# A hybrid decoder block on one core: split weights kept in DRAM for later blocks, LRU gates by heads of 64 rows, mixed input units, gelu in one operation

## The chip, the core and the metric

One NeuronCore of a Trainium2 chip runs the whole kernel. Its engines work side by side and wait for each other by semaphores: TensorE (PE, matrix products; its weight loads are listed as PEld), VectorE (DVE, elementwise), ScalarE (ACT, copies and functions), GpSimd (POOL, little used here) and SyncE (SP), whose queue issues every DMA in order. Tiles live in SBUF (128 partitions); matmuls accumulate in PSUM. The metric is the device time of one execution in microseconds; lower is better.

## The reference

The input is 2048 tokens of width 1024 in float32, one layer:

```
h = rmsnorm(x, norm_mix_g)
gate_b, gate_c, v, x_r, g = split(h @ w_in, [512, 1024, 1536, 2560])
y_conv = gate_b * causal_dwconv(gate_c * v, conv_w)
xr = causal_dwconv(x_r, rnn_conv_w) + rnn_conv_b
y_rnn = rg_lru(xr, w_a, b_a, w_x, b_x, lru_lambda) * gelu(g)
x = x + concat([rmsnorm(y_conv), rmsnorm(y_rnn)]) @ w_out
z = square(relu(rmsnorm(x) @ w_mlp_in))
out = rmsnorm(x + z @ w_mlp_out)
```

rg_lru computes two sigmoid gates, r and i, from xr with block-diagonal weights: 16 heads, each a 64 x 64 matrix for w_a and one for w_x. From r and lru_lambda it makes a decay a and a factor sqrt(1 - a*a), and scans h[t] = a*h[t-1] + factor*i*xr over the sequence.

## The kernel before

**Precision.** Each float32 operand of a product is split into a high part (a cast to fp32r, `w_hi`, `h_hi`, ..., on ACT) and the rest (a subtraction on DVE, `w_lo`, `h_lo`, ...): `split_into`, L152 to L154. A product is three matmuls, hi x hi, hi x lo and lo x hi (`passes`, L186).

**Blocks.** The sequence is cut into four blocks of 512 tokens, in two pairs. For each block `mixers` (L966) computes the two mixers and `w_out_rows` and `w_out_conv` (L992, L1014) the product with w_out; after both blocks of a pair the MLP runs on the pair with a seven-product Strassen scheme (`Up` and `Down`, L708 to L905).

**Units.** w_in and w_out are taken in units of 256 columns or rows, 1 MB each, 20 per block: x0 g0 x1 g1 x2 g2 x3 g3, then c, v, b for two column pairs, then oB0 to oB3 and oA0, oA1 of w_out. Each unit is 48 matmuls of 512 columns. `take` (L174) hands out a unit, issues the loads of the ones after it (`load_unit`, raw tiles of 512 KB from DRAM) and the splits of the next two (`split_unit`). Raw and split tiles share a pool of 15 slots of 4 KB per partition (`wp`), so a load waits until an older unit's slots are free. In every block the same 20 units are loaded raw and split anew.

**A mixer pair.** For each of four pairs `pr` of 128-channel groups, `lru_conv` (L550) copies the x unit's result out of PSUM, convolves it on DVE and splits it into xr_hi and xr_lo; `lru_gelu` (L584) makes the polynomial of the tanh gelu from the g unit's result; `lru_scan` (L598) does the gate products. `load_gates` (L272) builds two 128 x 1024 tiles, one for w_a and one for w_x, with two heads on the diagonal of each 128 x 128 square and zeros beside them; per 128 channels six matmuls (L610, accumulator `psri`) use all 128 rows. Then come sigmoids, tanh, exp and sqrt on ACT and the scan on DVE. In block 0 the results are scaled by `row` on DVE.

**Norms.** `next_part` (L929) prepares the next block's norm in steps; its step 8 spreads four scales over the partitions with a matmul (L380) into a PSUM tile `bc` of its own, and ACT copies that to `bcs`. `stats` (L532) sums squares over channels with four matmuls (L536) into a tile `sps`.

**What sets the order.** Outside of parts that are written out by hand, a scheduler orders each engine's instructions by estimated times; the program order sets what exists. Within an engine, instructions start in order, and a wait holds back all that is behind it. All tiles come from rings of slots: PSUM has four accumulators of two banks (`psp`).

**Start of the MLP.** `seq` (L1118) runs products 1 and 2 of three column slices first. Meanwhile `rest` (L1102) turns the last tiles of the second block and makes H6 and H5, and H7, H3 and H4 are split at steps 2, 3 and 4. `Up.drain` adds and squares the results (L789, L797, L801, square at L780) and stores them (`d_z`); `Down.fetch` loads them back, `Down.prepare` splits them.

Of the kernel before, what the change touches and what calls it, by code (L numbers as in the profile page):

```python
# [50 lines left out]
def block_kernel(  # L51
# [75 lines left out]
    units = []  # L127
    for b in range(NB):
        for pr in range(4):
            units.append(("x%d" % pr, src_col(w_in, COL_X + 256 * pr)))  # L130
            units.append(("g%d" % pr, src_col(w_in, COL_G + 256 * pr)))
        for pr in range(2):
            for nm, col in (("c", COL_C), ("v", COL_V), ("b", COL_B)):
                units.append((nm + str(pr), src_col(w_in, col + 256 * pr)))
# [17 lines left out]
    def split_into(hi, lo, src, lo_engine=None):  # L152
        nc.scalar.copy(hi, src)  # L153
        (lo_engine or V).tensor_tensor(lo, src, hi.bitcast(F32), SUB)  # L154
# [111 lines left out]
    def gate_tiles():  # L266
        raw = [temp("gate_raw", (P, NLRU, P)) for _ in range(2)]
        for r in raw:
            nc.gpsimd.memset(r, 0.0)
        return raw  # L270

    def load_gates(raw):  # L272
        res = []
        for src, r in zip((w_a, w_x), raw):
            sv = src[0].rearrange("(c e) i j -> e i c j", e=2)
            for e in range(2):
                nc.sync.dma_start(
                    r[64 * e : 64 * e + 64, :, 64 * e : 64 * e + 64], sv[e]
                )
            hi = temp("gate_hi", (P, NLRU, P), F32R)  # L280
            lo = temp("gate_lo", (P, NLRU, P), F32R)
            split_into(hi, lo, r)
            res.append((hi, lo))
        return res
# [34 lines left out]
    for nm, n in ROWS:  # L319
        nc.sync.dma_start(prow[o : o + n, :], srcs[nm])  # L320
# [161 lines left out]
    l_neg = cp.tile(L8, F32, name="l_neg")  # L482
    l_abs = cp.tile(L8, F32, name="l_abs")
    l_u = cp.tile(L8, F32, name="l_u")
    l_d = cp.tile(L8, F32, name="l_d")
    l_w = cp.tile(L8, F32, name="l_w")
    l_w2 = cp.tile(L8, F32, name="l_w2")
    l_s = cp.tile(L8, F32, name="l_s")
# [2 lines left out]
    V.tensor_scalar(l_neg, lam, -1.0, 0.0, MUL, MAX)
    V.scalar_tensor_tensor(l_abs, l_neg, 2.0, lam, MUL, ADD)
    nc.scalar.activation(l_u, l_abs, AF.Exp, scale=-1.0)
    V.tensor_scalar(l_d, l_u, 2.0, None, ADD)
    V.reciprocal(l_d, l_d)
    V.tensor_mul(l_w, l_u, l_d)
    V.tensor_mul(l_w2, l_w, l_w)
    V.tensor_scalar(l_s, l_w2, 2.0 / 15, 2.0 / 13, MUL, ADD)
    for n in (11, 9, 7, 5, 3, 1):
        V.tensor_mul(l_s, l_s, l_w2)  # L500
        V.tensor_scalar(l_s, l_s, 2.0 / n, None, ADD)
    V.tensor_mul(l_s, l_s, l_w)
    V.tensor_add(l_s, l_s, l_neg)
# [750 lines left out]
```

## Time and profile before

| | |
|---|---|
| median of three runs | 2193.27 us (2191.85 to 2193.27) |
| profiled execution | 2192.01 us |
| its span, first to last instruction | 2190.2 us |
| granted TensorE clock, mean | 0.997 |
| bytes moved by DMA | 334.10 MB, 153 GB/s in the mean |
| matmuls | 9634 |

The page gives for each engine the time in which it was busy, the groups of instructions by line and tile, and the chain of work that ended last. A group's row holds line, engine, operation, tiles written and read, shape and count, then total busy time and the mean of one in ns, then the idle time before them and what ended it. Matmuls overlap: one lasts longer than the distance to the next, so their pace is read from starts, as in the chain's pieces. The slices of the page show the clock in tenths, and 9 or more in all of them.

### The profile page before, as it was taken

The page shows a single profiled execution, that of the slowest core. Times are in us where ns is not written, and L with a number is a line of the kernel's source. Part 1 is how long each engine was busy: PE and PEld are TensorE (multiplying, and loading weights), DVE is VectorE, ACT ScalarE, POOL GpSimd, SP SyncE. Part 2 cuts the span into 40 slices and gives each one's busy share as a digit, 9 for nine tenths or more (in the row PEclk, how much of TensorE's full clock was granted, in tenths as well). Part 3 has the DMA queues.
Part 4 walks back from the last instruction along what each step waited for, and adds up shares of the span by engine and source line. Part 5 has one row for each costly group of instructions (what it writes and reads, how often), then busy time and mean ns, then how long its engine had stood idle before and what let it go on. Part 6 is the DMA issues. An engine that isn't in the chain of part 4 may idle for free.

```text
span 2190.2 us, 25124 instructions
## 1 busy us (share of the span) xinstructions
PE 2168.8 (99%) x9634; PEld 1793.4 (82%) x9634; DVE 1671.5 (76%) x1951; ACT 1033.0 (47%) x1341; POOL 52.0 (2%) x54
## 2 busy tenths in 40 slices
PE   9999999999999999999999999999999999999997
PEld 7888888887888888888888888888888888788886
DVE  7898678769757678778888876876886665887866
ACT  6764486534333333334478535774443333333343
POOL 0110001000000000000000000000000000000000
PEclk9999999999999999999999999999999999999999
DMA  7334533443453577444263424233335355854432
GB/s 250 105 117 154 183 106 125 146 133 108 148 177 116 203 270 257 154 154 145 89 210 93 158 97 163 87 127 142 106 118 200 116 186 198 304 195 154 132 100 77
DMA packets 179752, 334.10 MB, mean 153 GB/s; under 512 B 14672, under 2 KB 104880, under 8 KB 179632
## 3 DMA queue, kind: packets, MB, share of 16 engines
q1 hardware_dynamic: 179632, 332.49, 44.2%
q8 instruction: 76, 1.25, 0.2%
q14 instruction: 44, 0.36, 0.0%
HBM read 252.76 MB, written 79.69 MB: 152 GB/s over the span
## 4 chain that ended last, share of the span: by engine, by line
PE 88%; DVE 7%; DMA 2%; issue 1%; SPq 1%; ACT 0%; POOL 0%; DVEq 0%; ACTq 0%; POOLq 0%
PE dn L878 27%; PE up L764 23%; PE po L217 11%; PE ps_g L193 7%; PE ps_x L193 7%; PE ps_b L193 4%; PE ps_c L193 3%; PE ps_v L193 3%; PE psri L610 2%; DVE w_lo L154 1%; DVE H L154 1%; DMA x<-in_x_dram 1%; DVE x L922 0%; PE tps L1010 0%; DVE snap L789 0%
## 5 line engine op out<-in xcount | busy, mean ns | idle before, releaser
L764 PE MATMUL up<-H,w_hi 128*128 128x512 f32 x1792 | 552.4, 389 | 1.3 <-DVE snap L789 1.3
L764 PEld LDWEIGHTS up<-H,w_hi 128*128 128x128 f32 x1792 | 335.8, 188 | 72.0 <-issue 2.5
L878 PE MATMUL dn<-w_lo,z_hi 128*128 128x512 f32 x896 | 349.4, 390 | 1.9 <-DVE w_lo L154 1.9
L878 PE MATMUL dn<-w_hi,z_hi 128*128 128x512 f32 x896 | 349.3, 390 | 0.0
L878 PE MATMUL dn<-w_hi,z_lo 128*128 128x512 f32 x896 | 349.2, 390 | 0.0
L764 PE MATMUL up<-H,w_lo 128*128 128x512 f32 x896 | 348.7, 389 | 0.3 <-DVE w_lo L154 0.3
L153 ACT CAST w_hi<-w 128x1024 fp32r<-128x1024 f32 x156 | 164.2, 1052 | 339.2 <-PE up L764 159.4
L154 DVE TENSOR_TENSOR w_lo<-w,w_hi 128x1024 fp32r<-128x1024 f32 x156 | 190.5, 1222 | 111.6 <-ACT w_hi L153 39.3
L154 DVE TENSOR_TENSOR w_lo<-raw,w_hi 128x1024 fp32r<-128x1024 f32 x158 | 192.3, 1221 | 89.3 <-ACT w_hi L153 39.1
L153 ACT CAST z_hi<-z 128x1024 fp32r<-128x1024 f32 x112 | 117.8, 1051 | 200.1 <-PE dn L878 158.2
L153 ACT CAST w_hi<-raw 128x1024 fp32r<-128x1024 f32 x158 | 163.6, 1046 | 102.9 <-PE po L217 64.5
L878 PEld LDWEIGHTS dn<-w_lo,z_hi 128*128 128x128 f32 x896 | 168.6, 188 | 38.0 <-DVE w_lo L154 2.8
L764 PEld LDWEIGHTS up<-H,w_lo 128*128 128x128 f32 x896 | 168.2, 188 | 35.6 <-DVE w_lo L154 0.8
L878 PEld LDWEIGHTS dn<-w_hi,z_lo 128*128 128x128 f32 x896 | 168.6, 188 | 35.0
L878 PEld LDWEIGHTS dn<-w_hi,z_hi 128*128 128x128 f32 x896 | 168.5, 188 | 35.0
L154 DVE TENSOR_TENSOR z_lo<-z,z_hi 128x1024 fp32r<-128x1024 f32 x112 | 136.7, 1221 | 58.7 <-issue 26.1
L890 DVE TENSOR_TENSOR x<-dn,x 128x1024 f32<-128x1024 f32 x112 | 136.5, 1221 | 20.8 <-PE dn L878 20.6
L217 PE MATMUL po<-w_hi,y_hi 128*128 128x512 f32 x384 | 119.4, 392 | 0.0
L217 PE MATMUL po<-w_lo,y_hi 128*128 128x512 f32 x384 | 118.3, 389 | 0.0
L217 PE MATMUL po<-w_hi,y_lo 128*128 128x512 f32 x384 | 118.3, 389 | 0.0
L193 PE MATMUL ps_x<-h_hi,w_hi 128*128 128x512 f32 x240 | 93.5, 390 | 0.0
L193 PE MATMUL ps_g<-h_hi,w_hi 128*128 128x512 f32 x240 | 93.5, 390 | 0.0
(235 smaller groups left out, 3562.8 us busy)
## 6 DMA issues: line engine op xcount, KB each, us to landing
raw<-in_w_in_dram SPq DMA_DIRECT2D x112, 512.0 KB, 3.7
z<-d_z SPq DMA_DIRECT2D x112, 512.0 KB, 4.4
w<-in_w_mlp_in_dram SPq DMA_DIRECT2D x64, 512.0 KB, 6.7
d_z<-snap SPq DMA_DIRECT2D x64, 512.0 KB, 3.6
raw<-in_w_out_dram SPq DMA_DIRECT2D x48, 512.0 KB, 3.5
d_z<-z SPq DMA_DIRECT2D x48, 512.0 KB, 4.8
w<-in_w_mlp_out_dram SPq DMA_DIRECT2D x48, 512.0 KB, 3.6
x<-in_x_dram SPq DMA_DIRECT2D x20, 512.0 KB, 8.0
```

The source lines that it names most:

```text
L153: nc.scalar.copy(hi, src)
L154: (lo_engine or V).tensor_tensor(lo, src, hi.bitcast(F32), SUB)
L193: nc.tensor.matmul(ps[:, j, lo:hi], ws[k // 4][:, k % 4, j * P : (j + 1) * P], hs[:, k, lo:hi], start=k == 0 and i == 0, stop=k == KD - 1 ...
L217: nc.tensor.matmul(ps[:, half, :], ys[:, j, t * P : (t + 1) * P], ws[j][:, 0, half * 512 : (half + 1) * 512], start=first and i == 0, stop ...
L610: nc.tensor.matmul(pr_[:, half, :], ws[:, c, :], xsrc[:, j, :], start=i == 0, stop=i == len(pl) - 1,)
L764: nc.tensor.matmul(ps[:, j, :], ws[:, k, j * P : (j + 1) * P], hs(k), start=i in (1, 2, 5) and k == 0 and n == 0, stop=k == 3 and n == len ...
L878: nc.tensor.matmul(ps[t // 2][:, t % 2, :], zs[:, p, t * P : (t + 1) * P], ws[:, p, :], start=i in (1, 2, 5) and a == 0 and p == 0 and n == 0,
L890: V.tensor_add(xt[b, th, dh], ps[th], xt[b, th, dh])
```

## The change

It makes six edits.

1. **Kept splits.** When a unit is taken for the first time (units 3 to 22: the rest of block 0, and the first three of block 1), its four split tiles are stored to DRAM (`put_by`). A later block loads these four tiles straight into split slots, 2 MB per unit, with no cast and no subtraction, and looks two units ahead instead of three.
2. **Gates by heads.** One raw tile holds both weights: on rows 0 to 63 the even heads' w_a and w_x side by side, on rows 64 to 127 the odd heads' w_x and w_a. A matmul uses one half of the rows (64 of contraction, 128 results: 64 channels of r and 64 of i); the two halves alternate and have one PSUM bank each. The sigmoids work on 64 partitions, and b_x is needed with its halves swapped.
3. **Order of units.** x0 g0 x1 c0 g1 x2 v0 g2 x3 b0 g3 c1 v1 b1. The gate products follow the next pair's x unit; scan and convolution stand apart.
4. **gelu** in one ACT operation (`Gelu_apprx_tanh`) instead of square, tanh and three DVE operations.
5. **w_out.** The norm's spread and the sums of squares move from the mixers into the start of `w_out_rows`, where they use the fourth accumulator `po[3]` ahead of its own products; the splits of y are made one unit ahead.
6. **Start of the MLP.** For three of the eight slices relu and square run on ACT (two operations) instead of DVE (one). Two transposed tiles instead of one are left for the first MLP steps, H7, H3 and H4 are split at steps 4, 5 and 6, and the first Down operands are fetched a step earlier. In block 0 the split of the gates and the softplus of lru_lambda stand behind the first xr_lo.

```diff
+def KEEP(u, n):
+    return 3 <= u < n + 3
+    UNITS = ("x0", "g0", "x1", "c0", "g1", "x2", "v0", "g2", "x3", "b0", "g3", "c1", "v1", "b1")
+    def put_by(u, tiles):
+        cache[u % NU] = []
+        for part in tiles:
+            row = []
+            for t in part:
+                d = dp.tile(list(t.shape), F32, name="d_w")
+                nc.sync.dma_start(d, t.bitcast(F32))
+                row.append(d)
+            cache[u % NU].append(row)
     def load_unit(u):
...
+        his, los = [], []
+        for hi_d, lo_d in zip(*cache[u % NU]):
+            for to, d, nm in ((his, hi_d, "w_hi"), (los, lo_d, "w_lo")):
+                t = wtile(nm, shape, F32R)
+                nc.sync.dma_start(t.bitcast(F32), d)
+                to.append(t)
+        splits[u] = (his, los)
     def take(nm, ahead=AHEAD, lo_engine=None):
...
-        if ahead:
+        if ahead and not (u + ahead + 1 < len(units) and is_kept(u + ahead + 1)):
             load_unit(u + ahead + 1)
...
+        if KEEP(u, NU):
+            put_by(u, splits[u])
+    def load_gates():
+        r = temp("gate_raw", (P, NLRU, P))
+        for e in range(2):
+            for g, src in enumerate((w_a, w_x)):
+                col = 64 * ((g + e) % 2)
+                sv = src[0].rearrange("(c e) i j -> e i c j", e=2)
+                nc.sync.dma_start(r[64 * e : 64 * e + 64, :, col : col + 64], sv[e])
+        return r
     def lru_gelu(pr, h, row=None):
-            nc.scalar.copy(g, psg)
-            nc.scalar.activation(s, psg, AF.Square)
+            nc.scalar.activation(s, psg, AF.Gelu_apprx_tanh)
...
-        V.tensor_scalar(s, s, 0.044715, 1.0, MUL, ADD)
-        V.tensor_mul(s, s, g)
+    def lru_gates(pr, xr, xr_hl, gs):
-            for half, wg in enumerate(gates):
-                pl = passes(wg, xr_hl)
-                for i, (ws, xsrc) in enumerate(pl):
+            heads = (slice(0, 64), slice(64, P))
+            for i, (ws, xsrc) in enumerate(passes(gates, xr_hl)):
+                for e, own in enumerate(heads):
                     nc.tensor.matmul(
-                        pr_[:, half, :],
-                        ws[:, c, :],
-                        xsrc[:, j, :],
...
+                        pr_[:, e, :], ws[own, c, :], xsrc[own, j, :], start=i == 0, stop=i == 2
                     )
-            nc.scalar.activation(r[:, j, :], pr_[:, 0, :], AF.Sigmoid, bias=par("b_a", c))
-            nc.scalar.activation(gi[:, j, :], pr_[:, 1, :], AF.Sigmoid, bias=par("b_x", c))
+            for e, own in enumerate(heads):
+                other = heads[1 - e]
+                nc.scalar.activation(
+                    r[own, j, :], pr_[own, e, :], AF.Sigmoid, bias=par("b_a", c)[own]
+                )
+                nc.scalar.activation(
+                    gi[own, j, :], pr_[other, e, :], AF.Sigmoid, bias=par("b_x_swapped", c)[other]
+                )
     def lru_scan(pr, st, acc):
-        V.scalar_tensor_tensor(s, s, 1.0, g, ADD, MUL)
-        V.scalar_tensor_tensor(s, v, 0.5, s, MUL, MUL)
+        V.tensor_mul(s, v, s)
             def square(t):
-                V.scalar_tensor_tensor(t, t, 0.0, t, MAX, MUL)
+                if self.s < 3:
+                    nc.scalar.activation(t, t, AF.Relu)
+                    nc.scalar.activation(t, t, AF.Square)
+                else:
+                    V.scalar_tensor_tensor(t, t, 0.0, t, MAX, MUL)
     def mixers(b, h, early=None):
+        gs = lru_gelu(0, h, row)
+        psx = col_unit("x1", h)
+        st = lru_gates(0, xr, xs, gs)
+        xr = lru_conv(1, psx, row)
+        ysB[0], accB = lru_scan(0, st, accB)
+        xs = lru_split(xr)
+        gc = conv_c(0, h, row)
...
     def w_out_rows(b, ysB, accB, during):
             for t in range(NT):
+                if pr == 0 and t == 3:
+                    if b + 1 < NB:
+                        next_part(b + 1, 8, po[3][:, 0, :])
+                    rB = stats(accB, D, "B", po[3][:, 1, 0:NT])
+                    during(pr)
     def w_out_conv(b, ysA, accA, ahead, after, held=1):
-            if t:
+            if t and t - 1 < NT - held:
                 with tc.issue_after(root):
-                    after(t - 1, prev)
+                    after(t - 1, xs[t - 1])
-                if n == 1:
-                    rest(NT - 1, xs)
+                if n < 2:
+                    rest(NT - 2 + n, xs[NT - 2 + n])
-                if n == 2:
+                if n == 4:
                     for q in range(2):
                         V.tensor_tensor(r1[q], r1[2 + q], r1[q], SUB)
                     split_pair(7, r1[:2])
```

Where it moves instructions, three places. The first is PE in block 0, the gate products of the second pair (psri: accumulator; gate_hi_319 and gate_hi_325: w_a and w_x). Before, the first 128 channels:

```order
L610 MATMUL psri_697<-xr_hi_500,gate_hi_319 128x512
L610 MATMUL psri_697<-xr_lo_501,gate_hi_319 128x512
L610 MATMUL psri_697<-xr_hi_500,gate_lo_320 128x512
L610 MATMUL psri_697<-xr_hi_500,gate_hi_325 128x512
L610 MATMUL psri_697<-xr_lo_501,gate_hi_325 128x512
L610 MATMUL psri_697<-xr_hi_500,gate_lo_326 128x512
```

Now, the same channels and the next 128:

```order
L652 MATMUL psri_740<-xr_hi_516,gate_hi_356 128x512 x2
L652 MATMUL psri_740<-xr_lo_517,gate_hi_356 128x512 x2
L652 MATMUL psri_740<-xr_hi_516,gate_lo_357 128x512 x2
L652 MATMUL psri_751<-xr_hi_516,gate_hi_356 128x512 x2
L652 MATMUL psri_751<-xr_lo_517,gate_hi_356 128x512 x2
L652 MATMUL psri_751<-xr_hi_516,gate_lo_357 128x512 x2
```

The number of matmuls is the same; each x2 is a pair of the upper and the lower 64 rows (the listed size is that of the result).

The second is PE at the start of w_out in block 0 (po_1538 to po_1541: the four accumulators; diag: the norm's scales; v_488: the squares). These matmuls stood among the mixers' units before, in tiles bc and sps of their own:

```order
L253 MATMUL po_1540<-w_hi_1379,y_lo_1366 128x512 x2
L421 MATMUL po_1541<-diag_1452,ones_83 128x512
L253 MATMUL po_1538<-w_hi_1461,y_hi_1562 128x512 x2
L253 MATMUL po_1538<-w_lo_1462,y_hi_1562 128x512 x2
L253 MATMUL po_1538<-w_hi_1461,y_lo_1563 128x512
L582 MATMUL po_1541<-ones_83,v_488 128x1 x4
L253 MATMUL po_1538<-w_hi_1461,y_lo_1563 128x512
L253 MATMUL po_1538<-w_hi_1465,y_hi_1562 128x512 x2
L253 MATMUL po_1538<-w_lo_1466,y_hi_1562 128x512
L253 MATMUL po_1541<-w_hi_1375,y_hi_1365 128x512 x2
```

Nine matmuls of the next unit are put between the spread and the first product of po_1541, which starts that accumulator anew.

The third is DVE at the start of the first pair's MLP (snap: a product's result, whose addition, L789 before and L840 now, also frees an accumulator; w1 and s3: MLP weights and their sums; H5, H6, H7: operands). Before, the stretch that leads to the second such addition:

```order
L154 TENSOR_TENSOR H5_3727<-h0_3300,H5_3725 128x2x128
L1147 TENSOR_TENSOR r1_3574<-r1_3576,r1_3574 128x1024
L154 TENSOR_TENSOR H6_3723<-T2_3579,H6_3721 128x2x128
L154 TENSOR_TENSOR w_lo_3992<-w1_3929,w_hi_3991 128x1024
L735 TENSOR_TENSOR s3_3995<-w1_3514,w1_3890 128x1024
L1147 TENSOR_TENSOR r1_3575<-r1_3577,r1_3575 128x1024
L736 TENSOR_TENSOR w1_3890<-w1_3890,w1_3892 128x1024
L154 TENSOR_TENSOR H7_4030<-r1_3574,H7_4028 128x1024
L738 TENSOR_TENSOR w1_3514<-w1_3890,w1_3514 128x1024
L154 TENSOR_TENSOR H7_4031<-r1_3575,H7_4029 128x1024
L154 TENSOR_TENSOR w_lo_4037<-w1_3931,w_hi_4036 128x1024
L789 TENSOR_TENSOR snap_4024<-up_4040,snap_4024 128x1024
```

Now:

```order
L175 TENSOR_TENSOR H5_3788<-h0_3415,H5_3786 128x2x128
L783 TENSOR_TENSOR w1_3926<-w1_3926,w1_3928 128x1024
L175 TENSOR_TENSOR w_lo_4089<-w1_3967,w_hi_4088 128x1024
L785 TENSOR_TENSOR w1_3575<-w1_3926,w1_3575 128x1024
L1236 TENSOR_TENSOR r1_3635<-r1_3637,r1_3635 128x1024
L1236 TENSOR_TENSOR r1_3636<-r1_3638,r1_3636 128x1024
L840 TENSOR_TENSOR snap_4086<-up_4092,snap_4086 128x1024
L175 TENSOR_TENSOR w_lo_4123<-w1_3575,w_hi_4122 128x1024
L787 TENSOR_TENSOR w1_3577<-w1_3577,w1_3575 128x1024
L1242 TENSOR_TENSOR h0_3417<-h0_3417,T2_3639 128x1024
L1242 TENSOR_TENSOR h0_3419<-h0_3419,T2_3640 128x1024
L175 TENSOR_TENSOR H7_4161<-r1_3635,H7_4159 128x1024
```

The two splits of H7 have moved behind the second addition, and the square on DVE (L780) that followed each addition is gone.

More of the change, by code (lines that the diff above doesn't have):

```diff
@@ L127, in block_kernel @@
     units = []
+    UNITS = ("x0", "g0", "x1", "c0", "g1", "x2", "v0", "g2", "x3", "b0", "g3", "c1", "v1", "b1")
+    COLS = dict(x=COL_X, g=COL_G, c=COL_C, v=COL_V, b=COL_B)
     for b in range(NB):
[L129 to L134, printed above, removed]
+        for nm in UNITS:
+            units.append((nm, src_col(w_in, COLS[nm[0]] + 256 * int(nm[1]))))
         for pr in range(4):
@@ L153, in split_into @@
         nc.scalar.copy(hi, src)
-        (lo_engine or V).tensor_tensor(lo, src, hi.bitcast(F32), SUB)
+        return (lo_engine or V).tensor_tensor(lo, src, hi.bitcast(F32), SUB).ins
     def load_unit(u):
-        if u < len(units) and u not in raws and u not in splits:
+        if u >= len(units) or u in raws or u in splits:
+            return
+        if u % NU not in cache:
             raws[u] = load_tiles(*units[u][1], "raw", wtile)
+            return
+        shape = units[u][1][1]
+        his, los = [], []
[5 more added lines that the diff above has]
+        splits[u] = (his, los)
     def split_unit(u, lo_engine=None):
@@ L163, in split_unit @@
         load_unit(u)
+        if u in splits:
+            return
         shape = units[u][1][1]
@@ L264, in gain, with split_gates @@
         return g
[L266 to L284, printed above, removed]
+    def load_gates():
[6 more added lines that the diff above has]
+        return r
+    gates = []
+    def split_gates(r):
+        hi = temp("gate_hi", (P, NLRU, P), F32R)
+        lo = temp("gate_lo", (P, NLRU, P), F32R)
+        split_into(hi, lo, r)
+        gates[:] = hi, lo
     g_row = temp("g_row", (KD, P))
@@ L319, in block_kernel @@
     for nm, n in ROWS:
-        nc.sync.dma_start(prow[o : o + n, :], srcs[nm])
+        if nm == "b_x_swapped":
+            for e in range(2):
+                nc.sync.dma_start(
+                    prow[o : o + n, 64 * e : 64 * e + 64],
+                    srcs["b_x"][:, 64 - 64 * e : 128 - 64 * e],
+                )
+        else:
+            nc.sync.dma_start(prow[o : o + n, :], srcs[nm])
         off[nm] = o
@@ L472, in block_kernel @@
     load_unit(2)
-    gates = load_gates(gate_raw)
+    gate_raw = load_gates()
     split_unit(2)
@@ L481, in block_kernel, with softplus_begin, softplus_end @@
     L8 = [P, NLRU]
[L482 to L488, printed above, removed]
     sp4 = cp.tile(L8, F32, name="sp4")
     sp8 = cp.tile(L8, F32, name="sp8")
[L491 to L503, printed above, removed]
-    V.tensor_scalar(sp4, l_s, -4.0, None, MUL)
-    V.tensor_scalar(sp8, l_s, -8.0, None, MUL)
+    l_neg = cp.tile(L8, F32, name="l_neg")
+    l_u = cp.tile(L8, F32, name="l_u")
+    def softplus_begin():
+        l_abs = cp.tile(L8, F32, name="l_abs")
+        V.tensor_scalar(l_neg, lam, -1.0, 0.0, MUL, MAX)
+        V.scalar_tensor_tensor(l_abs, l_neg, 2.0, lam, MUL, ADD)
+        nc.scalar.activation(l_u, l_abs, AF.Exp, scale=-1.0)
+    def softplus_end():
+        l_d, l_w, l_w2, l_s = (cp.tile(L8, F32, name="l_" + n) for n in ("d", "w", "w2", "s"))
+        stt = V.scalar_tensor_tensor
+        V.tensor_scalar(l_d, l_u, 2.0, None, ADD)
+        V.reciprocal(l_d, l_d)
+        V.tensor_mul(l_w, l_u, l_d)
+        V.tensor_mul(l_w2, l_w, l_w)
+        V.tensor_scalar(l_s, l_w2, 2.0 / 15, None, MUL)
+        for n in (13, 11, 9, 7, 5, 3):
+            stt(l_s, l_s, 2.0 / n, l_w2, ADD, MUL)
+        stt(l_s, l_s, 2.0, l_w, ADD, MUL)
+        V.tensor_add(l_s, l_s, l_neg)
+        V.tensor_scalar(sp4, l_s, -4.0, None, MUL)
+        V.tensor_scalar(sp8, l_s, -8.0, None, MUL)
+    made_at = {}
     halo = cp.tile([P, NLRU, 3], F32, name="halo")
@@ L547, in stats, with lru_conv @@
         return r
[L550 removed]
+    def lru_conv(pr, psx, row=None):
         c0 = 2 * pr
[L552 removed]
         xr_in = wide("xr_in", 3)
@@ L952, in next_part @@
         elif n == 8:
-            nc.scalar.copy(bcs, spread(nxt["diag"], NT))
+            nc.scalar.copy(bcs, spread(nxt["diag"], NT, ps))
     def next_scale(b, q):
```

142 lines of the change are left out of this document (87 added, 55 removed).

## The prediction

> **What bounds the kernel now.** I read the page first, for which engine is full.
>
> ```profile
> span 2190.2 us, 25124 instructions
> PE 2168.8 (99%) x9634; PEld 1793.4 (82%) x9634; DVE 1671.5 (76%) x1951; ACT 1033.0 (47%) x1341; POOL 52.0 (2%) x54
> ```
>
> TensorE (PE) is busy for 99% of the span, so a faster DVE or ACT gives time back only where PE waits for it. Busy time of overlapping matmuls says little about their rate, so next comes the chain of work that ended last, inside the first block:
>
> ```profile
> 68.28 2.72 PE psri L610 x12
> 71.00 10.88 PE ps_g L193 x48
> ```
>
> The columns are start, length, and what ran. 48 matmuls in 10.88 us are 226.7 ns each, start to start, and the 12 gate matmuls (psri) in 2.72 us run at the same pitch. PE is a stream of 226.7 ns steps. Third, what PE waited for in the whole run (total us, times, longest):
>
> ```profile
> PE dn L878 <- DVE w_lo L154: 1.9, 1, 1.9
> PE start_x L447 <- ACT w_hi L431: 1.5, 1, 1.5
> PE up L764 <- DVE snap L789: 1.3, 3, 0.8
> PE tps L1010 <- DVE xs L354: 1.2, 1, 1.2
> PE start_x L416 <- POOL ones L229: 1.1, 1, 1.1
> PE psri L610 <- DVE xr_lo L154: 1.0, 1, 1.0
> PE ps_c L193 <- DVE w_lo L154: 0.3, 1, 0.3
> PE up L764 <- DVE w_lo L154: 0.3, 1, 0.3
> PE sps L536 <- DVE v L533: 0.2, 1, 0.2
> ```
>
> Without the two start_x rows, which the change doesn't touch, that is 6.2 us of waits in 2190. So two things can be won: PE steps that are no longer issued or run side by side, and at most these few microseconds. The profiled execution took 2192.01 us (span 2190.2 and 1.8 around it); the median of the three runs shown, 2193.27, is 1.3 above it. I sum against 2192.0 and add 1 at the end.
>
> **The gates: the term that decides.**
>
> ```profile
> L610 PE MATMUL psri<-xr_hi,gate_hi 128*128 128x512 f32 x64 | 24.8, 389 | 0.0
> L610 PEld LDWEIGHTS psri<-xr_hi,gate_hi 128*128 128x128 f32 x64 | 12.0, 188 | 2.6
> ```
>
> In the first row stand count, busy us, mean ns of one and idle before it. Three such groups of 64 are 192 gate matmuls, 192 x 0.2267 = 43.5 us of PE. The count stays 192, but each now uses 64 of the 128 rows, and the upper and lower half alternate, each with its own accumulator bank. No matmul of this shape is in the trace, so I bound it:
> - Both halves stream together, with nothing lost at the ends: 96 steps, 21.8 us saved.
> - A drain at each change between whole-array and half-array work. A matmul lasts 389 ns at a pitch of 227, so 162 ns drain behind its issue. 16 bursts x 2 ends x 0.162 = 5.2 us, leaving 16.6.
> - Weight loads as the limit. Each half needs its own, so a pair has two. If the 188 ns of the load row were its pitch, a pair would take 376 ns: 96 x 0.376 = 36.1, saving 7.4. The transposes speak for a shorter pitch:
>
> ```profile
> 257.03 1.03 PE L1010 MATMUL tps<-ident,xs 128*128 128x128 f32 x8
> 257.82 0.48 PE L193 MATMUL ps_g<-h_hi,w_hi 128*128 128x512 f32 x1
> ```
>
> Eight transposes, each with its own 128-column load, are through in 0.79 us, so loads can follow each other every 99 ns. Two make 198, below 227. This row is nearer than the duration of one load.
> - No overlap at all: 0 saved, and 5.2 lost with drains.
>
> I take overlap and half of the drains: 21.8 - 2.6 = **19.2 us saved**.
>
> The rows speak for a pitch of 227 per pair with a drain of up to 162 ns at each end. The Trainium skill, "TensorEngine Tiling (Array Packing)", Key Properties, speaks against the change: changing the tiling mode, not just the tile, drains TensorE. By that rule the whole 5.2 would fall due and the saving be 16.6. "TensorE: Matmul & The Clock Gate", Part 3, reports 3.07 times for four row tiles; as an estimate from that page, the same 77% of ideal for two tiles saves 43.5 x (1 - 1/1.54) = 15.2. No run here shows either yet.
>
> **Waits that go.** Of the 6.2 us:
> - psri 1.0 (start of block 0): DVE does two gate_lo subtractions and the small softplus operations ahead of xr_lo. One gate_lo goes and the rest now stands behind xr_lo: 1.0 gone.
> - up 1.3 + 0.3, and tps 1.2: DVE is the late one. At the first of the two places it works without a gap:
>
> ```profile
> 491.80 1.23 DVE L154 TENSOR_TENSOR w_lo<-w,w_hi 128x1024 fp32r<-128x1024 f32 x1 [0.97 <-PE up L764]
> 492.94 1.22 DVE L789 TENSOR_TENSOR snap<-up,snap 128x1024 f32<-128x1024 f32 x1
> ...
> 494.41 1.22 DVE L780 SCALAR_TENSOR_TENSOR snap<-snap 128x1024 f32<-128x1024 f32 x1
> ...
> 519.46 1.22 DVE L789 TENSOR_TENSOR snap<-up,snap 128x1024 f32<-128x1024 f32 x1
> ```
>
> From 492 to 522 it has no idle. Three L780 (1.2 us each) leave it for ACT, the splits of H7, H3 and H4 come two steps later, and the last two transposed tiles wait for their x behind matmuls: 2.8 gone. What could be late next is H6 and H5; their splits move ahead of those of H7.
> - dn 1.9: z and w_lo for the second Down step. Its z is fetched one step earlier, but DVE's sums stay. After it PE also runs at half pace for a while, 427 ns apart:
>
> ```profile
> 1878.41 0.63 PE L878 MATMUL dn<-w_hi,z_lo 128*128 128x512 f32 x1
> 1878.84 0.63 PE L878 MATMUL dn<-w_hi,z_hi 128*128 128x512 f32 x1
> ```
>
> Eight steps at 0.2 extra are 1.6, so 3.5 hang on this wait. I take half, 1.7.
> - ps_c and sps 0.5: gone, both places are rebuilt.
>
> Sum 1.0 + 2.8 + 1.7 + 0.5 = **6.0 saved**; bounds 0 and 7.8.
>
> **A wait that is new.** The norm scale (bc) and the sums (sps) now use the fourth w_out accumulator before its own matmuls. Nine matmuls of the next unit are put between, 9 x 0.227 = 2.0 us. In that time ACT must copy bcs and DVE read the sums; everything left of w_out queues behind it on PE.
>
> ```profile
> 142.66 0.59 ACT L953 COPY bcs<-bc 128x512 f32<-128x512 f32 x1 [0.38 <-PE bc L380]
> 165.31 1.05 PE L536 MATMUL sps<-ones,v 128*128 128x1 f32 x8 [0.20 <-DVE v L533]
> ```
>
> With idle engines the copy (0.59) and sums (1.05) fit to within a few tenths; with DVE behind by three or four operations of 1.2, as block 0 may have it, it is 4 us once. Bounds 0 and 6; I take 0.5 in each of four blocks, **2.0 lost**.
>
> **What lies beside PE, costed at nothing.**
>
> ```profile
> L153 ACT CAST w_hi<-raw 128x1024 fp32r<-128x1024 f32 x158 | 163.6, 1046 | 102.9 <-PE po L217 64.5 <-PE ps_v L193 15.5 <-PE ps_b L193 7.8
> L154 DVE TENSOR_TENSOR w_lo<-raw,w_hi 128x1024 fp32r<-128x1024 f32 x158 | 192.3, 1221 | 89.3 <-ACT w_hi L153 39.1 <-PE ps_v L193 13.6 <-PE ps_x L193 8.4
> L594 DVE TENSOR_SCALAR s<-s 128x1024 f32<-128x1024 f32 x16 | 11.0, 689 | 2.5 <-ACT s L590 2.5
> L595 DVE TENSOR_TENSOR s<-s,g 128x1024 f32<-128x1024 f32 x16 | 19.5, 1221 | 0.1
> L640 DVE SCALAR_TENSOR_TENSOR s<-s,g 128x1024 f32<-128x1024 f32 x16 | 19.4, 1215 | 2.3 <-ACT s L625 2.3
> L617 ACT ACT_TABLE_LOAD x16 | 20.5, 1283 | 0.3
> L617 ACT ACTIVATE r<-psri,prm 128x512 f32<-128x512 f32 x32 | 22.1, 690 | 0.2
> 44.00:246.00 202.00, 201.46 (x903) 166.12 (x904) 175.16 (x232) 118.16 (x165) 19.36 (x9) 1.00 0.39 126
> ```
>
> Keeping splits removes 114 casts (119 us of ACT) and 114 subtractions (139 us of DVE). The one-step gelu removes L594, L595 and L640, about 3.1 us of DVE per unit pair. Sigmoids on half the partitions are still 512 wide, so I price each at the same 690 ns: 64 become 128, 44 us more for ACT. Table loads (1283 ns) number 66 against 64 before. The last row (length; busy time of PE, PEld, DVE, ACT, POOL; clock; DMA share; GB/s) is block 0: PE 201 of 202 us, DVE 175, ACT 118. All of it is hidden by PE; were PE's cover gone, DVE would have 27 us of air there. The accumulators are read in time: x's copy stands ahead of the eight sigmoids on ACT, and a buffer comes round only two units (22 us) later.
>
> At the start, two more parameter DMAs (b_x swapped) stand on SP ahead of x1's raw weights.
>
> ```profile
> 20.09 0.25 SPq L320 DMA_DIRECT2D prow<-in_g_norm_conv_dram  x1
> 21.41 0.27 SPq L320 DMA_DIRECT2D prow<-in_g_norm_rnn_dram  x1
> ...
> 26.52 1.23 DVE L154 TENSOR_TENSOR w_lo<-raw,w_hi 128x1024 fp32r<-128x1024 f32 x1
> ...
> 31.49 0.39 PE L193 MATMUL ps_x<-h_hi,w_hi 128*128 128x512 f32 x1
> ```
>
> Such DMAs are at most 1.32 us apart here, so x1's first split, done at 27.75, comes by 30.4, still ahead of PE's 31.49: nothing. The second half's split, 2 us behind, is used 24 matmuls later.
>
> The added stores and loads also lie beside PE if they keep up.
>
> ```profile
> q1 hardware_dynamic: 179632, 332.49, 44.2%
> raw<-in_w_in_dram SPq DMA_DIRECT2D x112, 512.0 KB, 3.7
> d_z<-z SPq DMA_DIRECT2D x48, 512.0 KB, 4.8
> ```
>
> 44.2% of 2190 us for 332.49 MB is 2.9 us per MB with all engines. Block 0 gains 17 units x 4 x 0.524 = 35.7 MB of writes, 104 us. Its present share, 0.39 x 202 = 79 us, makes 183 of about 197. Later blocks read 2 MB per unit, 6.1 us of 10.9. A store waits on SP's queue for its unit's split, and the next raw loads queue behind it; these are issued some two units (22 us) ahead of use and land in 4 to 5.
>
> **Sum.** 2192.0 - 19.2 - 6.0 + 2.0 = 2168.8; plus 1 for the median, **2170**.
>
> **The rivals** (all with the 1 for the median, from 2193).
> 1. *The halves don't overlap.* For it: no row shows this shape. Gates 0 to +5.2, waits -4: 2189 to 2194. Against it: the halves share neither rows nor banks. 12%.
> 2. *Overlap, limited by weight loads* (376 ns a pair): -7.4 + 2.6 - 4 gives 2184, with no drain or all of it 2182 to 2187. The 188 ns speak for it, the 99 ns of the transposes against. 12%.
> 3. *Slower: stores starve the loads of block 0.* SP issues in order. If DMA works only 80% of the time, because the queue stands before a store whose split isn't done, 183 us of transfers need 229, 32 more than 197: 2202. It decides once the share of time in which SP keeps the engines fed falls below 183/197 = 93% and the lead of two units is used up. For it: the share of 0.39 more than doubles. Against: stores may trail into w_out, and a store's split was issued two units earlier. 9%.
> 4. *DVE's lateness stays*: the 6.0 aren't saved, 2176; with the 2.0 doubled, 2178. This lies inside the forecast's own range and has no chance of its own.
>
> **How the numbers follow.** Forecast 62%. Its own range is 2163 (no drain, all 7.8 saved, no new wait: 2193 - 21.8 - 7.8) to 2180 (full drains, half the waits kept, 6 at po: 2193 - 16.6 - 3 + 6). Rivals 12, 12 and 9%; 5% for less than 2163. The range 2158 to 2191 leaves out rival 3, some two thirds of rival 1 and a little below, 19% in all. A measurement of this kernel tells about 0.2%, 4.4 us, from no change. Faster by more than that: forecast, what is below it, and rival 2, 79%; within it: rival 1, 12%; slower: rival 3, 9%.
>
> **What would show it.** Chain: psri pieces of 12 matmuls in about 1.5 us rather than 2.72, and the next unit's matmul right behind. 2.7 there is rival 1, 2.2 rival 2. PE's waits: no psri, tps or up rows; a po row of a few tenths. Windows over block 0: DMA share about 0.9 with PE still full; a PE row that waits for raw or w_lo in 100 to 240 us would be rival 3. I am wrong if the two halves serialize, or if block 0 is no longer PE's.

## The result: 2174.3 us, 0.85% faster

The kernel after takes 2174.27 us (median of four runs, 2171.66 to 2175.45), the kernel before 2193.24 beside it (2191.85 to 2193.27). The ratio is 0.9915, with a 95% interval of 0.9903 to 0.9927. 2170 was predicted, with 2158 to 2191 as the range.

The page of the profile after (its execution took 2173.16 us):

```profile
span 2171.4 us, 25196 instructions
PE 2152.1 (99%) x9634; PEld 1773.1 (82%) x9634; DVE 1471.3 (68%) x1763; ACT 983.1 (45%) x1300; POOL 43.5 (2%) x50
...
q1 hardware_dynamic: 177648, 434.22, 54.8%
```

PE is as full as before, with the same 9634 matmuls. DVE does 200 us less and the DMA queue moves 102 MB more. What PE waits for (total us, times, longest):

```profile
PE po L421 <- DVE u L730: 3.3, 1, 3.3
PE start_x L488 <- ACT w_hi L472: 2.4, 1, 2.4
PE start_x L457 <- POOL ones L265: 1.1, 1, 1.1
```

None of the waits of before is left but the two at the start. One is new. The chain of work that ended last, at a burst of gate matmuls in block 1:

```profile
280.04 1.59 PE psri L652 x12
281.62 11.10 PE ps_c L229 x48
```

The 12 gate matmuls take 1.59 us, not 2.72: the halves do run side by side. But the unit behind them takes 11.10 instead of 10.88. PE at the new wait, in block 0:

```profile
178.16 0.61 PE L253 MATMUL po<-w_hi,y_lo 128*128 128x512 f32 x2
182.09 2.07 PE L421 MATMUL po<-diag,ones 128*128 128x512 f32 x2 [3.31 <-DVE u L730]
183.79 1.23 PE L253 MATMUL po<-w_hi,y_hi 128*128 128x512 f32 x2
184.81 0.92 PE L253 MATMUL po<-w_lo,y_hi 128*128 128x512 f32 x2
```

The same stretch as windows (length; busy time of PE, PEld, DVE, ACT, POOL; clock; DMA share; GB/s):

```profile
178.00:182.00 4.00, 0.78 (x4) 0.31 (x2) 3.90 (x4) 0.00 (x0) 0.00 (x0) 1.00 0.75 293
182.00:186.00 4.00, 3.91 (x10) 2.33 (x10) 2.88 (x5) 3.93 (x7) 0.00 (x0) 0.57 0.02 9
```

After a pause of 3.3 us the granted clock is 0.57 for four microseconds, so the wait costs about half as much again.

To see where time goes, I cut each run where TensorE's first matmul of the next stage starts in the trace. "mix" is a block's mixers, "out" its product with w_out, "Down" runs to the last matmul. The two Up stages of the MLP, which never differ by over 1.1 us, are left out; all is in us, from the profiled execution.

| kernel | mix 0 | out 0 | mix 1 | out 1 | Down 1 | mix 2 | out 2 | mix 3 | out 3 | Down 2 | span |
|---|---|---|---|---|---|---|---|---|---|---|---|
| before | 176.1 | 68.8 | 166.0 | 68.8 | 305.0 | 165.0 | 68.8 | 165.1 | 70.4 | 308.1 | 2190.2 |
| after | 169.3 | 75.8 | 160.6 | 70.1 | 304.6 | 159.6 | 70.6 | 160.6 | 68.9 | 304.4 | 2171.4 |
| gates_whole | 173.1 | 72.3 | 164.2 | 69.8 | 304.6 | 163.2 | 70.6 | 164.2 | 68.9 | 304.4 | 2182.3 |
| no_keep | 169.6 | 79.3 | 160.6 | 75.0 | 304.6 | 159.6 | 78.3 | 160.6 | 74.7 | 304.4 | 2194.5 |
| keep_alone | 185.5 | 70.9 | 166.1 | 70.4 | 306.8 | 165.0 | 68.8 | 165.1 | 70.4 | 306.6 | 2203.2 |
| gelu_late | 167.9 | 74.1 | 160.6 | 70.2 | 304.6 | 159.6 | 70.6 | 160.6 | 68.9 | 304.4 | 2168.3 |
| both_late | 168.1 | 72.6 | 160.6 | 70.2 | 304.6 | 159.6 | 70.6 | 160.5 | 68.9 | 304.4 | 2167.1 |
| fetch_late | 167.9 | 76.0 | 160.6 | 70.2 | 306.8 | 159.6 | 70.6 | 160.5 | 68.9 | 308.2 | 2176.1 |

Read by rows: the blocks after the first gained 5.4, 5.4 and 4.5 us in the mixers; "out" 2 took over 1.8 us of work that stood in the mixers before (spread and sums), and "out" 1 grew by 1.3 though one transposition of 0.9 us left it for Up (edit 6), as one left "out" 3; the last Down gained 3.7. **Block 0 gained nothing**: 176.1 + 68.8 and 169.3 + 75.8 are both 245. The row of no_keep shows the slowest of its ten executions (2196.35 us, median 2192.68) and so overstates its loss by some 3.7.

### The profile page after: what moved, and what is told of

It is laid out like the page before. It is cut to its first block, busy times and chain, and to the rows that moved or that the text cites. A ratio compares the mean times of both kernels' runs of the same rounds, so it can differ in the third digit from the quotient of the medians.

```text
span 2171.4 us, 25196 instructions
## 1 busy us (share of the span) xinstructions
PE 2152.1 (99%) x9634; PEld 1773.1 (82%) x9634; DVE 1471.3 (68%) x1763; ACT 983.1 (45%) x1300; POOL 43.5 (2%) x50
## 4 chain that ended last, share of the span: by engine, by line
PE 91%; DVE 4%; DMA 2%; ACT 2%; issue 1%; SPq 0%; POOL 0%; DVEq 0%; ACTq 0%; POOLq 0%
PE up L811 28%; PE dn L929 27%; PE po L253 12%; PE ps_x L229 6%; PE ps_g L229 6%; PE ps_c L229 3%; PE ps_v L229 3%; PE ps_b L229 3%; PE psri L652 1%; DVE xr L617 1%; DMA raw<-in_w_in_dram 1%; PE tps L1098 1%; PE start_x L488 1%; DMA xT<-in_x_t_dram 1%; DVE x L973 0%
## 5 line engine op out<-in xcount | busy, mean ns | idle before, releaser
L608 DVE TENSOR_SCALAR xr<-xr_in,prm 128x512 f32<-128x512 f32 x32 | 17.3, 550 | 115.3 <-ACT xr_in L601 115.2
L229 PE MATMUL ps_x<-h_lo,w_hi 128*128 128x512 f32 x240 | 93.4, 389 | 0.0
```

The costliest lines, as they stand in the source:

```text
L229: nc.tensor.matmul(ps[:, j, lo:hi], ws[k // 4][:, k % 4, j * P : (j + 1) * P], hs[:, k, lo:hi], start=k == 0 and i == 0, stop=k == KD - 1 ...
L608: V.tensor_scalar(xr[:, j, :], xr_in[:, j, 0:TB], par("rnn_conv_w", c), par("rnn_conv_b", c), MUL, ADD,)
```

## The experiments

### What the gates are worth

**gates_whole.** Each gate matmul takes all rows, on the same tiles and in the same order, so that r and i are sums over two heads instead of one head's product.

```diff
-    pr_[:, e, :], ws[own, c, :], xsrc[own, j, :], start=i == 0, stop=i == 2
+    pr_[:, e, :], ws[:, c, :], xsrc[:, j, :], start=i == 0, stop=i == 2
```

> Kernel after, but every gate matmul takes all 128 rows (the same 192 matmuls, tiles, sigmoids and order; r and i are then sums over two heads instead of one head's product). Only the overlap of the halves and the changes of row use go. If the trace of after is read rightly, a burst of 12 takes 2.72 us again and the unit behind it 10.88 instead of 11.10: 0.91 per burst, 16 bursts, 14.6 us slower than after, about 2189. By the term of the prediction (half drains) it would be 19.2 slower, 2193; with the full drains of 0.162 per end, 16.6. If the gates brought nothing and the waits all of it: within 4 us of after.

Measured: 2183.35 us (2182.57 to 2184.19), ratio to before 0.9957 (0.9941 to 0.9974). Against after that is 9.1 us, less than each of the three sums and more than the waits alone would leave. The chain shows the burst as it was before:

```profile
280.28 2.72 PE psri L652 x12
283.00 10.88 PE ps_c L229 x48
```

The table explains the rest. In all four blocks the mixers are 3.6 to 3.8 us longer, 14.6 us together, as the first reading had it. In block 0, "out" is then 3.5 us shorter: PE comes later to the place where it waits for DVE. So the gates are worth 14.6 us of PE's time, and 9 (by the medians) to 11 (by the profiled spans) of the kernel's. About half of the change's gain has other sources.

**whole_ahead** and **whole_between** add one whole-row matmul per burst, ahead of it (j == 0) or in its middle (j == 1):

```diff
+    if j == 1:
+        nc.tensor.matmul(
+            pr_[:, 0, :], gates[0][:, c, :], xr_hl[0][:, j, :], start=True, stop=True
+        )
     for i, (ws, xsrc) in enumerate(passes(gates, xr_hl)):
```

> Kernel after with one extra matmul on all 128 rows ahead of each burst of gate matmuls (16 in all, into the bank that the first gate matmul then overwrites). It adds 16 steps and no change of row use: 0.227 per burst, 3.6 us in all. The burst in the chain of work goes from 1.59 to about 1.82. This is the control for the next run.

> Kernel after with the same extra whole-row matmul, now in the middle of each burst, between its two 128-channel groups: 16 steps and one more change from half rows to whole and back in each burst. If a pair of changes costs 0.40 to 0.45 us, as the starts around the bursts in the trace of after say, a burst takes 2.2 to 2.3 us and the run is 10 to 11 us slower than after, 6.4 to 7.2 slower than the run with the extra matmul ahead. If changes cost nothing and the loss at the bursts has another reason (the start of a stream, weight loads): 1.82 per burst and 3.6 us, as in the control.

Measured: 2174.93 and 2180.10 us, one execution each, so the reading rests on the traces. The chain at the same burst, ahead and between:

```profile
279.14 0.23 PE psri L651
279.37 1.59 PE psri L656 x12
280.96 11.11 PE ps_c L229 x48
```

```profile
279.57 0.90 PE psri L656 x6
280.47 0.43 PE psri L651
280.90 0.89 PE psri L656 x6
281.79 11.11 PE ps_c L229 x48
```

Ahead the burst takes 0.23 + 1.59 = 1.82 us, between 0.90 + 0.43 + 0.89 = 2.22. The same matmul at another place costs 0.40 more. Over the mixers of block 2, whose start and end no other difference touches, the sums are 160.5, 162.1 and, without the extra matmul, 159.6: 0.23 and 0.64 per burst. One more change from halves to whole rows and back costs **0.41 us**. That is most of the 0.45 which a burst loses in after: 1.59 + 11.10, where 6 + 48 steps of 226.7 ns would take 12.24.

**halves_in_turn** takes three matmuls of one half, then three of the other.

```diff
-    for i, (ws, xsrc) in enumerate(passes(gates, xr_hl)):
-        for e, own in enumerate(heads):
+    for e, own in enumerate(heads):
+        for i, (ws, xsrc) in enumerate(passes(gates, xr_hl)):
```

> Kernel after with the gate matmuls in another order: three of the upper half, then three of the lower, twice per burst, in place of alternating. If only neighbours in TensorE's queue run side by side, three of twelve pair up (9 steps instead of 6): 2.27 us per burst instead of 1.59, 10.9 us slower in all. If TensorE keeps a queue for each half of the rows and looks past a neighbour: 1.59, no change.

Measured: 2177.28 us, one execution. The first theory is wrong:

```profile
284.06 1.60 PE psri L652 x12
285.66 11.10 PE ps_c L229 x48
```

TensorE's queue holds three of one half and then three of the other, and still the two of a pair start 10 ns apart (3 to 4 ns in after). The order in the queue doesn't decide, at least over three matmuls. The mixers of blocks 1 to 3 take what they take in after; the difference lies in block 0 (171.0 and 78.2). There 1.6 us are in the start, which the edit doesn't touch, and the wait for DVE was followed by a second pause, of 0.6.

### Why block 0 gained nothing

DVE reads the last mixer accumulator (ps_b, line L730) late, and its slot is that of po's fourth accumulator. What ScalarE did ahead of that in after:

```profile
142.43 0.68 ACT L657 ACTIVATE r<-psri,prm 64x512 f32<-64x512 f32 x1
143.12 1.28 ACT L639 ACT_TABLE_LOAD   x1
144.41 1.06 ACT L639 ACTIVATE s<-s 128x1024 f32<-128x1024 f32 x1
145.48 1.28 ACT L660 ACT_TABLE_LOAD   x1
146.77 0.68 ACT L660 ACTIVATE gi<-psri,prm 64x512 f32<-64x512 f32 x1
```

Between the first and the second of eight sigmoids stands the gelu, with two table loads: 3.6 us by which the other sigmoids, the exps and with them DVE come later. DVE stands idle meanwhile (the first of its waits ends with PE's ps_c, because the order there puts gc ahead of gi):

```profile
148.89 1.23 DVE L698 TENSOR_TENSOR gc<-ps_c,row 128x1024 f32<-128x1024 f32 x1 [4.20 <-PE ps_c L229]
151.71 1.23 DVE L663 TENSOR_TENSOR gi<-gi,xr 128x1024 f32<-128x1024 f32 x1 [1.59 <-ACT gi L660]
155.72 1.22 DVE L677 SCALAR_TENSOR_TENSOR v<-r,v 128x1024 f32<-128x1024 f32 x1 [1.65 <-ACT r L671]
...
180.81 1.23 DVE L730 TENSOR_TENSOR u<-ps_b,u 128x1024 f32<-128x1024 f32 x1
```

**gelu_late** (pair 3 of block 0 alone), **split_late** and **both_late**, the two edits together:

```diff
-    nc.scalar.activation(v, v, AF.Sqrt, scale=-1.0)
+    root = nc.scalar.activation(v, v, AF.Sqrt, scale=-1.0).ins
+    if late:
+        with tc.issue_after(root):
+            nc.scalar.activation(s, s, AF.Gelu_apprx_tanh)
```

```diff
-    for v in range(u + 1, u + ahead + 1):
+    for v in range(u + 1, u + (ahead if splits_ahead is None else splits_ahead) + 1):
         split_unit(v, lo_engine)
...
-    ysA[1], accA = conv_b(1, h, accA, u, row)
+    ysA[1], accA = conv_b(1, h, accA, u, row, 1 if b == 0 else None)
```

> Kernel after; in block 0 the gelu of the fourth pair stands on ScalarE behind that pair's sqrt instead of between its first and second sigmoid. Theory: block 0's po wait (3.3 us, with the half pace behind it 5.2) is DVE's lateness, and DVE is late because ScalarE's sigmoids and exps of the fourth pair stand behind the gelu and two table loads (3.6 us). Then DVE reads ps_b 2.5 to 3 us earlier, the wait falls to under 1 us and no half pace follows: block 0 3.5 to 5 us shorter, about 2170. Rival: DVE has too much work in block 0 anyway (it reads ps_b at the same time within 1 us): no change, 2174.

> Kernel after; in block 0 the split of the second w_out unit is issued one unit later, so that one subtraction of 1.2 us less stands ahead of the read of ps_b on DVE. If that queue decides: the po wait goes from 3.3 to about 2.1 us, 1.2 to 2.5 us in all (2172 to 2173). If the wait hangs on the results that ScalarE delivers: unchanged, 2174; if the later split is then itself late, a new wait at the second w_out unit, up to 2 us slower than after.

> Both edits of the two runs before, in one kernel. If DVE's lateness in block 0 is the whole cause, no po wait is left there and block 0 is 5 us shorter than in after: about 2169. If the wait comes back elsewhere in block 0 (DVE has the same work to do before block 1 starts): within 2 us of after.

Measured, against 2193.02 us for before on that chip: gelu_late 2169.35 us (2168.47 to 2170.12; ratio 0.9895, 0.9880 to 0.9909), split_late 2175.72 (2175.09 to 2176.71; 0.9924, 0.9909 to 0.9939), both_late 2169.17 (2168.89 to 2170.47; 0.9895, 0.9880 to 0.9910). In gelu_late the wait for u is gone and a smaller one stands behind it:

```profile
175.36 1.23 DVE L734 TENSOR_TENSOR u<-ps_b,u 128x1024 f32<-128x1024 f32 x1
...
177.24 1.02 PE L421 MATMUL po<-diag,ones 128*128 128x512 f32 x2
...
181.31 0.57 ACT L1008 COPY bcs<-po 128x512 f32<-128x512 f32 x1
...
181.93 1.05 PE L582 MATMUL po<-ones,v 128*128 128x1 f32 x8 [1.38 <-ACT bcs L1008]
```

The lines are DVE, PE, ACT and PE. DVE reads ps_b at 175.36 instead of 180.81, of which 1.4 us come from an earlier start of the whole stream. On DVE the waits of 4.20, 1.59 and 1.65 have become 3.36 (for gi) and 1.65, and one of 1.17 behind them (for ACT's v) is gone: 3.6 us less, the length of the gelu with its two loads. So the gelu's place is the cause of DVE's lateness, and the theory holds. The saving is smaller than the wait: the sums now wait 1.4 us for the copy of bcs, which stands behind casts and y_hi on ACT, so "out" 0 falls only from 75.8 to 74.1, and to 72.6 with both edits. split_late alone took the wait from 3.3 to 2.0 us as that theory said, but then made PE wait 1.7 us for y_hi behind it, and the time did not fall. Between the profiled spans of gelu_late and after lie 3.1 us (4.9 between the medians), and 1.4 of them are in "mix" 0, in the start, which the edit doesn't touch; some 1.7 are the edit's. All four executions of gelu_late are faster than all of after; both_late adds nothing that can be told from it.

### What the kept splits are worth

**no_keep** and **keep_alone**: the change without edit 1, and edit 1 alone on the kernel before.

```diff
 def KEEP(u, n):
-    return 3 <= u < n + 3
+    return False
```

> Kernel after without kept splits: every block loads raw weights and splits them, as the kernel before did (no stores of splits, 114 casts and 114 subtractions more). Theory: that work lies beside TensorE, and the waits of before went by the new order of units and by what moved at the start of the MLP: within 3 us of after, block by block. Rival: the splits were what made DVE late in blocks 1 to 3 and at the start of the MLP: 5 to 8 us slower, with waits on w_lo back. Third: the stores of block 0 cost something that the trace of after hides: block 0 alone is faster by over 2 us.

> Kernel before with edit 1 alone (kept splits, nothing else). Theory: the casts and subtractions lie beside TensorE in that order of work, whose waits are 6.2 us in all, of which some 5 hang on DVE: 2187 to 2193. Rival: kept splits are worth there what they are worth in the kernel after, 18 us: 2175. Third: the stores of block 0 hold up its loads: slower than 2195.

Measured: no_keep 2192.68 us (2190.76 to 2196.35; ratio to the 2193.02 of before 0.9999, 0.9990 to 1.0009), keep_alone 2204.79 (2203.34 to 2208.45) against 2191.63 for before (ratio 1.0064, 1.0049 to 1.0079). So the same edit saves 18.4 us in one kernel and costs 13.2 in the other, and the first theory falls in both places. The largest waits of no_keep:

```profile
PE po L582 <- ACT bcs L1004: 10.1, 3, 4.2
PE po L253 <- DVE ys_B L590: 3.0, 1, 3.0
PE po L421 <- DVE u L730: 2.5, 1, 2.5
```

All three are at the place that edit 5 made; on w_lo, as the rival had it, there is one of 0.6. The mixers of blocks 1 to 3 take 160.6, 159.6 and 160.6 us with kept splits and without; only "out" grows, by 4.9, 7.7 and 5.8, and by 3.5 in block 0, which is thus not faster without the stores, as the third theory had it. The spread on PE and ACT's rows in block 1 of no_keep, and below them PE and ACT around the same copy in after:

```profile
418.72 1.02 PE L421 MATMUL po<-diag,ones 128*128 128x512 f32 x2
...
417.76 1.07 ACT L569 ACTIVATE cv<-u 128x1024 f32<-128x1024 f32 x1 [8.51 <-DVE u L730]
418.73 1.03 ACT L174 CAST w_hi<-raw 128x1024 fp32r<-128x1024 f32 x1
419.66 1.05 ACT L174 CAST H<-h 128x1024 fp32r<-128x1024 f32 x1
420.61 1.05 ACT L174 CAST w_hi<-raw 128x1024 fp32r<-128x1024 f32 x1
...
423.83 0.58 ACT L1004 COPY bcs<-po 128x512 f32<-128x512 f32 x1
```

```profile
414.96 1.02 PE L421 MATMUL po<-diag,ones 128*128 128x512 f32 x2
...
416.30 0.56 ACT L1004 COPY bcs<-po 128x512 f32<-128x512 f32 x1
...
416.92 1.05 PE L582 MATMUL po<-ones,v 128*128 128x1 f32 x8
```

In after the copy is through 1.9 us after the spread starts, and the sums find it done. Without kept splits DVE has four subtractions more ahead of L730, so ACT stands for 8.51 us until DVE has made u, and then has two casts more ahead of the copy, which starts 5.1 us after its spread. ACT works in order, so the small copy that PE needs waits for casts that PE doesn't need yet.

keep_alone gains nothing in blocks 1 to 3 (166.1, 165.0, 165.1 against 166.0, 165.0, 165.1), although DVE is busy for 97.9 us in block 1's mixers instead of 126.8. Of its loss, 13.0 us between the profiled spans, 11.5 are in block 0: 1.5 at the start, which the edit doesn't touch, and the rest at one place. Here are ACT's row in before, ACT's rows in keep_alone and then PE's:

```profile
170.14 2.55 ACT L519 ACTIVATE y_hi<-s,prm 128x512 fp32r<-128x512 f32 x4
...
180.44 1.06 ACT L563 ACTIVATE cv<-u 128x1024 f32<-128x1024 f32 x1 [5.06 <-DVE u L720]
182.84 0.20 ACT L591 COPY xr_in<-halo 128x6 f32<-128x6 f32 x1 [1.35 <-DVE cv L566]
184.88 1.04 ACT L175 CAST h_hi<-xT 128x1024 fp32r<-128x1024 f32 x1 [1.84 <-DVE xT L425]
185.84 1.33 ACT L556 ACTIVATE y_hi<-s,prm 128x512 fp32r<-128x512 f32 x2
...
186.61 1.22 PE L254 MATMUL po<-w_hi,y_hi 128*128 128x512 f32 x2 [7.52 <-ACT y_hi L556]
```

In the kernel before, ACT made y_hi at 170.14, ahead of the square of cv. With the added instructions the scheduler put it behind that square and behind the next block's h_hi, and PE stood for 7.5 us. ACT had stood idle for 5.06 us just before that square, and DVE read ps_b no later than before (179.19 and 179.09), so it is the order on ACT. None of PE's waits names a load or a store, so the third theory got the sign right with the wrong mechanism.

**no_keep_own** and **own_tiles** undo the place of edit 5, without kept splits and with them.

```diff
+        part(6)
         yB = split_y(ysB[0], "g_norm_rnn", 0)
+        rB = stats(accB, D, "B")
         u = conv_v(1, h, gc, row)
-        part(6)
+        part(8)
         ysA[1], accA = conv_b(1, h, accA, u, row)
...
-                    if b + 1 < NB:
-                        next_part(b + 1, 8, po[3][:, 0, :])
-                    rB = stats(accB, D, "B", po[3][:, 1, 0:NT])
```

> The kernel without kept splits, and edit 5 undone too: the norm's spread and the sums of squares have tiles bc and sps of their own again, spread and sums stand between the last mixer units. Theory: the 18 us that went without kept splits are the price of edit 5's wait (the sums wait for ACT's copy of bcs, which then stands behind casts): with own tiles they come back but for a few waits on splits, 2175 to 2181. Rival: ACT and DVE are late at the start of w_out whatever stands there, since they have the casts and subtractions to do: waits of the same size under other names, 2188 or more.

> Kernel after with edit 5's place undone in the same way, kept splits left in. Theory: with kept splits edit 5 costs nothing in blocks 1 to 3 (within 1 us each), and block 0 still waits for the fourth accumulator, which DVE's late read of ps_b holds: within 3 us of after. Rival: spread and sums in po[3] cost their wait of 1 to 2 us in each block even so: 3 to 6 us faster than after.

Measured: 2255.53 us (2255.44 to 2257.05; ratio 1.0293, 1.0275 to 1.0310) and 2251.36 (2250.31 to 2253.66; 1.0275, 1.0260 to 1.0290). Both miss every expectation, through my choice of place. PE's waits in own_tiles:

```profile
PE sps L582 <- DVE v L576: 72.2, 4, 22.8
```

In the new order of units the fourth pair's scan comes so late that its sums, put ahead of v1, hold PE for 16 to 23 us in each block. With that pause in each block ACT and DVE catch up, so the two runs can't answer what they were made for, whether ACT and DVE would be late at w_out without edit 5. They do show that in edit 3's order the sums can't stand ahead of v1; a place between that and edit 5's wasn't tried.

### The Down operands

**fetch_late** fetches the first Down operands where the kernel before did.

```diff
-                        if i == 2:
-                            downs[0].fetch(1, 0, Z)
-                            downs[0].fetch(1, 1, Z)
...
                     if i == 6:
-                        downs[0].fetch(2, 0, Z)
-                        downs[0].fetch(2, 1, Z)
+                        downs[0].fetch(1, 0, Z)
+                        downs[0].fetch(1, 1, Z)
                     if i == 5:
+                        downs[0].fetch(2, 0, Z)
+                        downs[0].fetch(2, 1, Z)
                         downs[0].sums(0)
```

> Kernel after with the first Down operands fetched where the kernel before did (one step later). If that fetch is what removed the wait of 1.9 us at the second Down step with the half pace behind it: the last Down stage takes 308.1 us again instead of 304.4, 3.7 slower in all. If the kept splits or the squares on ScalarE removed it: unchanged.

Measured: 2177.91 us, one execution; what PE waited for at Down:

```profile
PE dn L929 <- DVE w_lo L175: 3.7, 2, 1.9
```

The last Down takes 308.2 us again, 3.8 more than in after, and the first takes 306.8 instead of 304.6. The same wait of 1.9 us cost 2.2 in one pair and 3.8 in the other: in the second, half pace followed (a granted clock of 0.59 in the four microseconds behind it; 1.00 in the first). The fetch is what removed it.

## Why the prediction came out right, step by step

The forecast case came true: the halves overlap, the waits of before are gone, and a wait at po is new. The sizes were off in both directions. Between the two profiled executions 18.9 us went: 14.6 by the gates and 10.6 by waits, less 5.2 at po ("out" 0 grew by 7.0, of which 1.8 is the work moved there) and 1.2 at the start. The gates brought 4.6 less than predicted and the waits 4.6 more; that these two cancel is luck.

- **The gates, 19.2 predicted, 14.6 measured.** "I take overlap and half of the drains" is the step that failed. The overlap is full (pairs 230 ns apart), but a change of rows costs 0.41 us there and back, more than the whole of 2 x 0.162 that stood as the upper bound of the drains: 16 x 0.41 is 6.6 us instead of 2.6. The rule of the Trainium skill, "TensorEngine Tiling (Array Packing)", Key Properties, that a change of tiling mode drains TensorE, was right against the half that I took, and the 16.6 worked out with full drains was nearer. The estimate from the Trainium skill's "TensorE: Matmul & The Clock Gate", Part 3, 15.2, was nearest, but by luck: whole_between shows a loss for each change of rows and not a fixed share of the ideal.
- **Waits that go, 6.0 predicted, 10.6 measured.** I priced them by the rows of the waits, which count idle time only, and took half of the 3.5 at Down. Measured by stages: Down 3.7 and 0.4, block 0's mixers 2.5 (6.8 and the 1.2 of the start, less 3.7 of the gates and 1.8 of moved work), Up 2.9 and block 3 1.5 (with the transposition of 0.87 that edit 6 moves from "out" 1 and 3 into each Up counted where it stood), blocks 1 and 2 together 0.4 slower. Idle starts at the modelled end of the matmul before, so from start to start a wait costs more than its row, and where half pace follows, up to twice as much. fetch_late shows both at Down (2.2 and 3.8 for 1.9); the other waits were not undone one by one.
- **The new wait at po, 2.0 predicted as 0.5 in each block, 5.2 measured, all of it in block 0.** Its bounds of 0 and 6 held, and "with DVE behind by three or four operations of 1.2, as block 0 may have it, it is 4 us once" names the place. But PE waits there for neither the copy nor the sums, which the term priced: it waits for the accumulator itself, because DVE reads ps_b too late. "The accumulators are read in time" is the step that failed. That it was the gelu between two sigmoids that made DVE late, gelu_late shows. The prediction counted the 27 us of air that DVE had in block 0, and not the waits that DVE itself has in them.
- **Kept splits, costed at nothing.** "All of it is hidden by PE" holds for the mixers of blocks 1 to 3, in keep_alone and no_keep alike. It fails at the start of w_out: there the same casts and subtractions decide whether edit 5's wait is nothing or 3 to 4 us. The prediction worked out each edit against the profile of before, so it priced the kept splits without edit 5 and edit 5 without asking what its wait would be if the casts were still there. 18 us of cover were in neither term, and the sum came out because the change makes both edits at once; that, too, is luck.
- **The rivals.** No overlap and a limit by weight loads are out by the 1.59 us. Stores that starve loads: block 0's DMA share rose from 0.39 to 0.83 (about 0.9 was worked out), and none of PE's waits names a transfer. Without the stores (no_keep) PE takes the same 137.8 us from x1's first matmul to w_out in block 0. Single transfers did get slower: the chain in block 0 has a store of 8.62 us and a load of 8.85, where 4 to 5 were counted.

```profile
42.00:242.00 200.00, 196.69 (x891) 159.93 (x890) 163.97 (x226) 129.60 (x177) 14.51 (x9) 0.99 0.83 305
```

- **The start.** 1.2 us more than in before, and 1.4 more than in gelu_late, belong to no edit: the wait of start_x is 2.4 us there, 1.5 in gelu_late and 1.2 in fetch_late, with the same instructions, and half pace follows it for longer.

Left open: how much of the 10.6 us each of edits 3, 4 and 6 brought outside Down, whether the wait at w_out without kept splits is edit 5's place alone, and whether a version with kept splits and an earlier scan could take spread and sums back into the mixers.

## What to carry to other kernels

Price a group of edits in pairs: work that a full engine hides can become the cover of another edit's wait, and a trace of before shows neither. Where half-row matmuls replace whole ones, gather them, since each change to halves and back costs about two steps of 512 columns. And a wait of two or three microseconds on TensorE should be counted from start to start with the half pace behind it, not by its row of idle time.

## What the hardware showed unasked

- Matmuls on different halves of the rows pair up even when three of one half are queued ahead of three of the other (1.60 us for 12, against 1.59).
- A change from halves to whole rows and back, for one matmul, costs 0.40 to 0.41 us on top of that matmul; a burst of 12 half-row matmuls among whole-row ones loses 0.45.
- After a pause on TensorE the clock may be granted at half for some microseconds: 0.57 in the window behind the 3.3-us wait. It isn't the pause's length alone that decides: in fetch_late one wait of 1.9 us was followed by it and another wasn't. The Trainium skill, "TensorE: Matmul & The Clock Gate", Part 1, tells of a free-running window of some 3.4 us without work; the dependence on where the pause falls agrees, while half pace after less than 2 us is shorter than that figure.
